# A two-layer diffusion trunk on one core: a second searched order of the same instructions on the five engine queues

## The chip, the cores and the metric

The kernel runs on one core of one Trainium2 chip. The metric is the device time of one execution, in microseconds (us); the median of several runs counts. The names of the engines in this text are those of the profile: PE (TensorE's matmuls; PEld its weight loads), DVE (VectorE), ACT (ScalarE), POOL (GpSimd) and SP (SyncE, which here only issues DMA transfers).

## The reference, cut to what matters

512 latent tokens and 256 context tokens of width 1024 go through two layers. Each layer has a mixer and a gated feed-forward part with a three-tap convolution along the tokens (ConvFFN, width 2816). The mixer of layer 0 is neighbourhood attention on a 64-wide grid for half of the width and spatial gating for the other half; that of layer 1 is retention in both directions. Every part is normed before and after, and shift, scale and gate come from the conditioning vectors (adaLN). Only the latent tokens leave the last layer.

```python
for i in range(DEPTH):
    ctx_out = i < DEPTH - 1
    mod_lat = (silu_c @ ada_w[i] + ada_b[i])[:, None, :]
    mod_ctx = (silu_cc @ ada_w[i] + ada_b[i])[None, None, :]
    sh1, sc1, g1, sh2, sc2, g2 = jnp.split(mod_lat, 6, axis=-1)
    ...
    h_lat = modulate(rmsnorm(x, norm_g[i, 0]), sh1, sc1)
    h_ctx = modulate(rmsnorm(xc, norm_g[i, 0]), csh1, csc1)
    y_ctx, y_lat = hybrid_na_sgu(...)  or  retention_mixer(...)
    x = x + g1 * rmsnorm(y_lat, norm_g[i, 1])
    h = modulate(rmsnorm(x, norm_g[i, 2]), sh2, sc2)
    x = x + g2 * rmsnorm(conv_ffn(h, ...), norm_g[i, 3])
    # the same for xc while ctx_out
```

All inputs and the output are float32.

## The kernel before, in words

**Precision.** Every large product is made of three passes on TensorE: each operand is split into a high and a low part, and high·high, high·low and low·high are added in PSUM (`mm3`, lines 277 to 280). `split` (lines 233 and 234) makes the parts: ACT copies the rounded high part (L233), DVE subtracts it from the source for the low part (L234). So each weight block of 128x1024 that comes by DMA costs ACT about 1.05 us and DVE about 1.22 us before its matmuls can run. The feed-forward and retention projections use block products of a Strassen kind (tiles px, py, pz, xv, yv, zv), whose sums are made on DVE.

**Stages.** The tokens are six tiles of 128 rows: 4 and 5 are context, 0 to 3 latent. From the start: first norms and the modulation vectors (`ad`, L328, native float32 matmuls on blocks `ar` of the modulation weights; transposes of the normed tiles `ht`, L2136), spatial gating and attention of layer 0 (to about 345 us), its output projection and the norms behind it (to 430), the feed-forward part of layer 0 (to 875), the norms between the layers (875 to 945; tiles with the letter c), retention (to 1400), the norms behind it (1400 to 1430; letter d), the feed-forward part of layer 1 (to 1757) and the last norms.

**Norms.** `ssq` (L493) squares half a row tile on ACT and sums it. `rms` (L498) adds the two sums in a 128x1 operation on GpSimd, and `rsq` (L479) raises the result to −1/2, also 128x1 on GpSimd. DVE and ACT then scale the tile (L515 at the start, L531, L543 and L544 later). Each norm is thus a chain ACT, GpSimd, GpSimd, DVE or ACT, and behind it PE transposes the result (`ht` L642 and L2136, `htc` L577) and `split` makes `hb` or `h0c`/`h1c`.

**Background work.** The remaining modulation vectors are made on DVE in small steps (`ada_half`): GpSimd clears an accumulator `acc` (L407), a row of the bias comes by DMA (L408), and DVE adds scaled weight rows to it (L416, 256 operations of 754 ns). Sums of retention weights for the block products are made by DMA alone: copies within DRAM and adding DMAs (`weight_sums`, L380; tiles tv and tq, 512 or 256 KB each), issued by SP and GpSimd and used only in the second layer.

**The order of the work.** `queue()` (lines 2152 to 2174) sets it. The program is built in some order; then the string ORDER (lines 51 to 185) is unpacked. It holds, for each of the five queues, one permutation of that queue's instructions, as the distance of each instruction from the one before it. Each instruction is tied to its predecessor in the permutation, so that the program is emitted in that order:

```python
at += 1 + (z // 2 if z % 2 == 0 else -(z + 1) // 2)
if last is not None:
    self.tc.add_manual_dep(lane[at], last.name, sync, reason="queue")
last = lane[at]
```

The dependency is one of order only; it adds no semaphore. The waits between engines follow from what the instructions read and write. An instruction at the head of a queue that waits holds up everything behind it in that queue, and DMA issues stand in the queues of SP, GpSimd and ACT like any other instruction. The permutations were made by a search program outside the kernel, with a model of the engines; the kernel holds only its result.

**Lines that the steps below touch.** First loads `first_load` (called on line 2208, tiles xn04, xn05) and `first_x` (L515); `ada_first` (L328); `ada_half` (L407, L408, L416); `rms` and `rsq` (L498, L479); `split` (L233, L234); `weight_sums` (L380).

Of the kernel before, what the change touches and what calls it, by code (L numbers as in the profile page):

```python
# [18 lines left out]
P = 128  # L19
D = 1024  # L20
KD = 8
NT = 4
NC = 2
TL = 512
TC = 256
FF = 2816
# [25 lines left out]
c-oD82e>3xb>_LZLRY8i?&_TTb-$c*&N<JE6W+XelXKRLq#0?XQ2?QcB!r|<0wj`z1j3jo8zF&=iN@I8{V+Dci@{)w*WNYjyx#v*zmW!P?{1G?b$4~$Tl  # L52
b#upZ}bDOGJ3-4&6a2`2+auBJw4Y2})BU$iI=Hlaui0C-U+ox{i}xkNq3PV?-w2`D<0J6>$~9?E`O~sNY$ir_wHJr;{hBulMcZZQ|`>YprL?JPp*<?lkW
bbdQ+t<O{mCzb>kifu{v|w$<GsioJ6u4fQyjyF+-tDIOB7R63IEbVdGFd`G-PJk6KYTzn2~=;DQz(@|Pl?u>0bD>ep)2C3`h2gC=(v8nFe-G|82-9z*_@
mWEoo)+pEe?+`X96m(Ul<g#o78jz~zB9Diow$)G(OvGPfn49d+eP~<Ii}{x=}D*3eG587WF#RK)gr?gWvM|PF><>@ZdYYh<w&e@WVnW?oT{jNXy43qS?O
FdQCc=RMY)nuswkf#N>Mh$GpiWP^;PVnf&PkkEPh~)rir#>`sfHG(}F8X&d_p64qeTiDWffCh_0vUnKNe-wdH3MD^-<5v5D~;*AmHwhV>XFcVD<zJxe#!
g~h51h5T}T{+3ItR9jj`yQ*t0(Q17IEkLhrt!?FabCW7D0I5j4IrPdZTBoksRl?<af?MbzagN7VN?Z8M>>OpX5Q(jg^0`u~pwg99Oe4K{uDX6Fjw{z^@>
IXNLbM}~xoxEuYNQFvzM^d%(tw)p7WattQ)4wf^xNV^QA#~~_U_qB8#UE69qrA>H*8H$PucgW=!deLrD15MN^hko1t=eeN%{jdE=s|=2Kw!><5~+gI^|v
QussI+9&gZcx!HnkJHBeyY)C#6y_i1JXB!pmJytZ~5Px|@oX0T|Eq;S!iq>b4+wOvB|0(_+4q-$$-*oeV(9O4r`nlPrMrvv1f7`6#kzpbXnp&r<R@(eX9
YoE9V{04E)i?AUA!_M4(bCgRY|{`d#7K0x7uGtogo%uejx8(>duVxhga(I-gW%teR8{_n$MgxwiovU{mK`sdXrt-&I|YU@Ni(-@p+Y`1gFAJZzHyqGY^K  # L60
Y%ULKFmHa2xtWBzq<qWK=`tgNc7D_4&nsOqEcjkcO<bawK@$=<cP+B$0ai1@iU(?Z+le=g`0v`8aAfe$?<j#C5QxAPt1Ct~?g9R33SLlrkH_7A{D>imHl
=5p0@v&U1jw@@vW9Q&W*zY1!Zrn%H&^P#5%-IO|N>0cEui9^|2o)oj65q?tR;}f3{xb=zm3eq5_EuRv16ea(F{DgQz93(n;fG1qBeFx<WbnXqYOtzljP;
8krIb{@uWKwNrj;b@%M4pilu_DL$JbMaW%h38fwc4NGF6a*Nh*%ipFXyha&piknxfg%$74H#@QMBjp#rhS9;x7gLLgc?9{#C5M2Zw(VbF*`^J8*bT{H`G
1ABeZhw@Ln^ZFD1jMXbW`j?>jwCquy{+E!ILdG2Ac?|Jcn{EnEJZloO*(>HHklY^6u=e7|=Z@3Y1dZ(=J^Isg^*gZC?!c0Q9%ZFq&W<6hb5vE{~V{x#Nu
0LNi0ipwt(G5fwsdr?9cJ;z95-g&9`{~-(!XggSGi1DZ#sDNxs+vl?wIyWZ(KbFiPJ=~vAbO`bOn`Ps@d0tan1f1ZrtcJYh|{N7K#vQ5;N9X;F-Qw=?%K
MdoOiz}=<h}AYl8k&?7JfV8EAdx<oWT>qdRxkCxpA#T6|G_MCjx6d2x-9O79Td^D30~b@4U8&-21NF>VWJ`0VCYnKK66a_N>!0|Wg79}x6mL5B{rgLeiw
A`Q@)vu8Tk<L7!`5+4-<{o4U6bi-4^q35`H6MY=_IB}A0y$qr4S7a}Ia)_?Gs;lw}qK(}|YdhZ((XV_;xfm|k2O1eq+U(P@c+MHm!9Yjg=Pe<2<`|$mN7
<4$8#AInjy2UlQL6or_?Z|S`WNwI!Qh%t;@qbN)XqP~9)nnu9~YP#ZpCh1;3oKMxn?K~ydE!YU><bg?3o>eI86pCd?VSnc~yPGTe^pT(x@A#-DiV3#c^N
2Dw#!GEP|fJ(xUPxAdXG4WU>lCSKdP_t7dtMwr!=E@(PFu&8rv>Rc|%GTBYV>BH7x;5C<b_u`-@Ic3-EFvoW?JM5)Vr;<5cF%9?$r-zQp{ZLz5d57qcdH
>u7RkK0>XX8$Y3MW7-FocS&DGd6g8fOB3?qa9EHwc!wER}Xy_Up?ytF&6SHsm3tHcv5K&v862!!IPni92H&?4ZH3Y_X*k#!R#WkImk9ljyl>q+WkCfIEU  # L70
GJkLc%dx3&eXt;a1~K`a&E%+Y&A!M<H=e0*Yx?iUjiM30M)izMReGQ2MIBSBvi)crkCcSZL6K-?v(4h`HRD?ced1qktdPtbP-4E-qgv8S(>I(`Nsf)MZv
ynPN=)I)vszYtH#-Obgzn>pa{-PZ@2Fu3hIw)?J#y(j6|an`Gc`$Tj@5dD-`+C#4k(myReBZ$w>5-sMscjd_KayM61B$CE+;{9T9&J{tF2kg;~I#tV+NI
+_PdSkUBkr*E7qRC(wyda9`#$KH4?t#6sMFKCkt<kPTlHMo3D#(56AbBEXv;jwLYb`6Kq!*(jT1_aE`{4@|86AIzxJx`JQXT8NCf5L}@x<NYTzL?Y1!kO
vu(z=6A<^5!TwA3J@~;74f;DVLUN-ecXtNO>HoAjG{RrtZt&)1Wd&bGvGl^(S3p<&M#sY=>^Y9#CeW0A;?b&A9OXFSd2C`3YncvIC+McA2$c3F9k=Eghs
-|k^9}zGH0NZIyBbqB=OM|&M3VD@SJg}pRa$Cz&giu&*dj`D4U>_mN0z{Y<5w?&3ZNCv7Kx@%4$)Uc}tnM+<p-q<?;VI>mPPV60brflwa`nbBtMLi&qQ>
Q=x{BTqc+R%1Nva%a1azgT(xQP_ym!~=SSuxa3teEt{S=Zk*1u!0$iv~pk;W#53t+^9q7bV<I4^CU`H1)}L0b{;)pSa|OPq~Ha=Uxu<xP#|ZZ_NYV{aEu
BNDw$(8(w>H?WFaNsiqknUFU52zi{<g|gCIohw)3#n5fG-P9PGp!x(Gzz7*kv|1a$oNWE5%*!0W-PII34UL~%S|*Gbv6w31TcP0{gJ>0V;!@3DwNw*=Vj
HLyxY`}8q9x8Ml6AG9B0z?CY?0=ZhoM#&Y>1)9EUeHNs9S4En3}Vs1)1PkxR6{J8@(d-PA~~8Z5$h=p-}jW*f|BQKZH~u{3H$_dA`AxW?!3$Io|Y?cv3t
pEJ`Io=<<b7IOh-e%(765r%}5tr#qTyF3+>7sb*@}NY0sB2q3q(uvkl>{<hX37<thyPwhq5V36TbkW8Du9~xq8O>d`xbZdP2C^a|N6evQYprexq+vC~s3
1(s&yNA75nCI|ZV32Jr+uC+%fc;A?TWW~(!8Rh%2)x>xu34%=ph%XwDP6j)k&^LP_v&k6gZ7>-jv)UY@g)I9`kL53&`(`JY`DP&?XUy<gxmGB*s=X_5hl  # L80
ZQ=z+<hcfk`>s?P>m%Tjt-(1I7Af`CTH8W%X&G7ahv(ozH9GYY(k=P`_m@|VO{h2c*c@k+=9hC(TJ*se~AxLMtz`zbOH6pL2t=_p;e2vhMRlvKft%|voz
_r`=&V$Cfbbf|>^1OYV`UyDXy7PP)=-MLx|$%Vop@Xs<%Eocj}5~{qNxxj**h4wUuo3k7wW~oH7okpT|B(0Ce$&OllCpJXGd{XS~2~3CfnpeaN0(=mp;B
hgz=tmkh<wrIdGzLB15kH4gIHxb><{01Kqg7iJc4r1oojyfpDL*}91t+I6xTugv?i=;A7xEMNd?C=BpBUc(^rb{8=C!-Td6&5CEaxx{ND6^ybokj|5fR-
u5r8XM{au~rlof0*%eqEs+2s!aHU@`k>*goMgAIerMr)YTj=Z0O*?uY@x8bPXpKD9_%t+KrxsJ&i#u@TcMXQgZ`Ho5tB6Tm-c{1c5qFRnXDbts=gOW{I&
~CVHc;|2h^S;#(f?fCSr^Nsb1jviP%)p^q!DIJ`kY3w%W+z-AeC+r!Hkf#GJB~c>DDG_qnIok;yVOu>qLR%q!qL`nW+=`PIvS~f&|x4*9c_0wFyl1f-d;
aBJkv--wryRc?1{c~H$}7f1<6er`5KeG1m~Oxj#@kFlfyfhk@-ig)IRE~I`DSZ`K{TwGnuEdtu*AavYBv2xi?u3{nk{2;JBE@3`di|J=hEYIy>6{bMyeU
QVodrFs0`Z(<|G|w~3jV<}n(s=njYasAROPv&QEGn}0ym7hniX-2C}A-|$E(;I~>bwA7~8uC8?G_55FWdL{<=r@5RH{ySS!L<30ZlVWd)e&KeJp=52FZr
# [2265 lines left out]
```

## Time and profile before

| | |
|---|---|
| median of 3 runs | 1772.27 us |
| lowest and highest | 1771.36 and 1775.65 us |
| the profiled execution | 1771.19 us, its span 1769.4 us |
| granted TensorE clock, mean over the span | 0.996 |
| busy: PE, PEld, DVE, ACT, POOL | 1731.5, 1563.9, 1434.4, 1122.4, 448.2 us |
| moved by DMA | 330.6 MB, mean 187 GB/s |
| instructions in the trace | 29634 |

The span runs from the first to the last record of the profiled execution; its own time is 1.8 us longer. Busy times add up instructions of one engine, overlapping ones once. An instruction's row gives its start, its length, engine, line, operation, output and inputs, and in brackets the idle time of its engine before it and what ended that. Rows of waits give, for an engine and line, for which producer it waited, the sum, the count and the longest. A window's row gives its length and each engine's busy time within it.

### The profile page before, as it was taken

What the parts mean: (1) busy time and instruction counts of PE and PEld (TensorE: products, weight loads), DVE (VectorE), ACT (ScalarE), POOL (GpSimd) and SP (SyncE); (2) the same over time, 40 slices, a digit from 0 to 9 for tenths busy, and PEclk for the clock granted to TensorE, in tenths of its full rate; (3) what the DMA queues carried; (4) which work ended last, traced back from release to release, by engine and by line L of the source; (5) the groups of instructions that cost most, each with busy time, mean ns of one, the idle gap of its engine ahead of it and who ended that gap; (6) DMA issues with size and microseconds to landing.
All of it is one profiled execution on the core that took longest, in us unless ns stands there. A gap on an engine that the chain in (4) does not pass through costs nothing.

```text
span 1769.4 us, 29634 instructions
## 1 busy us (share of the span) xinstructions
PE 1731.5 (98%) x11108; PEld 1563.9 (88%) x11108; DVE 1434.4 (81%) x2408; ACT 1122.4 (63%) x2046; POOL 448.2 (25%) x570
## 2 busy tenths in 40 slices
PE   7999999999999999999999999999999999999998
PEld 3798888789999899999889999999999889999997
DVE  3887787899888899878998677567657899998887
ACT  6633567786655565665675566566666677767774
POOL 1111344232143333232231131222121110222222
PEclk9999999999999999999999999999999999999999
DMA  8555584679799999999972465656564425787773
GB/s 299 153 163 177 162 200 107 192 217 240 223 205 231 222 246 229 270 230 250 316 206 71 175 172 155 148 133 163 120 151 144 174 103 169 194 219 186 177 159 125
DMA packets 121292, 330.59 MB, mean 187 GB/s; under 512 B 14222, under 2 KB 36238, under 8 KB 120476
## 3 DMA queue, kind: packets, MB, share of 16 engines
q1 hardware_dynamic: 63004, 233.73, 39.5%
q0 software_dynamic: 55840, 86.57, 29.7%
q10 hardware_dynamic: 2304, 8.39, 1.2%
q8 instruction: 87, 1.43, 0.3%
q14 instruction: 57, 0.47, 0.1%
HBM read 256.29 MB, written 98.30 MB: 200 GB/s over the span
## 4 chain that ended last, share of the span: by engine, by line
PE 81%; DVE 7%; ACT 4%; DMA 3%; POOL 3%; issue 2%; DVEq 0%; ACTq 0%; SPq 0%; POOLq 0%
PE px L277 10%; PE wf L278 4%; PE wf L279 4%; PE wf L280 4%; PE xv L277 4%; PE py L277 4%; PE px L280 1%; PE px L278 1%; PE px L279 1%; PE yv L277 1%; PE py L278 1%; PE py L280 1%; PE py L279 1%; PE ug L278 1%; PE wr L278 1%
## 5 line engine op out<-in xcount | busy, mean ns | idle before, releaser
L416 DVE SCALAR_TENSOR_TENSOR acc<-ar,cs,acc 128x512 f32<-128x512 f32 x256 | 188.0, 754 | 9.8 <-DMA acc<-in_adab_row 7.4
L2039 POOL DMA_DIRECT2D yf<-yp x64 | 55.7, 940 | 258.4 <-ACT yp L2035 226.6
L2035 ACT COPY yp<-wf 128x512 f32<-128x512 f32 x118 | 68.6, 584 | 70.5 <-PE wf L280 68.6
L277 PE MATMUL px<-hs,wc 128*128 128x384 f32 (+1 forms) x480 | 112.0, 309 | 0.8 <-ACT pre L1879 0.8
L277 PE MATMUL px<-blk,wb 128*128 128x384 f32 (+1 forms) x480 | 109.0, 308 | 0.0
L1892 DVE SCALAR_TENSOR_TENSOR cv<-pre,cw,cv 128x769 f32<-128x769 f32 (+1 forms) x88 | 77.6, 884 | 27.8 <-ACT cv L1891 27.5
L1891 ACT ACTIVATE cv<-pre,cw 128x770 f32<-128x770 f32 (+1 forms) x88 | 81.3, 926 | 19.3 <-DVE pre L1884 14.0
L277 PEld LDWEIGHTS px<-hs,wc 128*128 128x128 f32 x480 | 82.5, 188 | 6.7 <-ACT pre L1879 1.9
L277 PEld LDWEIGHTS px<-blk,wb 128*128 128x128 f32 x480 | 81.8, 188 | 4.7 <-ACT pre L1879 0.4
L1879 ACT ACTIVATE pre<-px 128x256 f32<-128x256 f32 (+2 forms) x160 | 54.3, 368 | 43.7 <-PE px L277 30.5
L2039 POOL DMA_DIRECT2D yd<-yp x48 | 47.4, 1020 | 124.7 <-ACT yp L2035 122.1
L1895 DVE SCALAR_TENSOR_TENSOR cv<-pre,cw,cv 128x769 f32<-128x769 f32 (+1 forms) x88 | 77.4, 884 | 1.3
L277 PE MATMUL px<-hs,wd 128*128 128x384 f32 x240 | 72.0, 338 | 0.0
L277 PE MATMUL py<-blk,wc 128*128 128x384 f32 x240 | 69.6, 337 | 0.0
L2039 POOL DMA_DIRECT2D yd<-ypg x48 | 45.7, 1006 | 86.5 <-ACT ypg L2035 73.4
L233 ACT ACTIVATE wb<-s 128x512 fp32r<-128x512 f32 x80 | 48.6, 627 | 22.1 <-PE px L277 19.1
L233 ACT ACTIVATE wc<-q 128x512 fp32r<-128x512 f32 x80 | 49.0, 629 | 17.6 <-PE px L277 6.9
L234 DVE TENSOR_TENSOR wb<-s,wb 128x512 fp32r<-128x512 f32 x80 | 54.6, 688 | 4.7 <-ACT wb L233 4.3
L234 DVE TENSOR_TENSOR wc<-q,wc 128x512 fp32r<-128x512 f32 x80 | 54.6, 688 | 4.3 <-ACT wc L233 4.0
L278 PE MATMUL wf<-fo,g 128*128 128x512 f32 x144 | 54.6, 397 | 1.2 <-ACT g L233 1.2
L280 PE MATMUL wf<-fo,g 128*128 128x512 f32 x144 | 55.5, 395 | 0.0
L279 PE MATMUL wf<-fo,g 128*128 128x512 f32 x144 | 55.2, 395 | 0.0
(1735 smaller groups left out, 6895.0 us busy)
## 6 DMA issues: line engine op xcount, KB each, us to landing
ar<-in_adaw SPq DMA_DIRECT2D x96, 512.0 KB, 4.9
yf<-yp POOLq DMA_DIRECT2D x64, 256.0 KB, 4.8
tv<-in_ret_vg SPq DMA_DIRECT2D x28, 512.0 KB, 6.1
yd<-yp POOLq DMA_DIRECT2D x54, 256.0 KB, 6.3
yd<-ypg POOLq DMA_DIRECT2D x54, 256.0 KB, 7.0
tv<-in_ret_vg POOLq DMA_DIRECT2D x14, 512.0 KB, 10.0
tq<-in_ret_qk SPq DMA_DIRECT2D x14, 512.0 KB, 6.2
tv<-tv POOLq DMA_DIRECT2D x14, 512.0 KB, 8.1
```

Of the source, the lines that this page charges most:

```text
L233: self.S.activation(hi, src, AF.Copy)
L234: self.V.tensor_tensor(out=lo, in0=src, in1=hi.bitcast(F32), op=ALU.subtract)
L277: mm = lambda *p, **k: self.T.matmul(*p, skip_group_check=True, **k)
L278: mm(out, lhs[0], rhs[0], start=first, stop=False)
L279: mm(out, lhs[0], rhs[1], start=False, stop=False)
L280: mm(out, lhs[1], rhs[0], start=False, stop=last)
L416: V.scalar_tensor_tensor(out=acc[s], in0=raw[:, kk * 512 : kk * 512 + 512], scalar=self.cs[:, 8 * s + k : 8 * s + k + 1], in1=acc[s], op0= ...
L1891: S.activation(d, s, AF.Identity, scale=w1, bias=b)
L1892: V.scalar_tensor_tensor(out=d[:, 1:W], in0=s[:, 0 : W - 1], scalar=w0, in1=d[:, 1:W], op0=ALU.mult, op1=ALU.add)
L1895: V.scalar_tensor_tensor(out=d[:, 0 : W - 1], in0=s[:, 1:W], scalar=w2, in1=d[:, 0 : W - 1], op0=ALU.mult, op1=ALU.add)
L2035: S.copy(v, ps)
L2039: G.dma_start((yd[t] if first else y[t])[:, o], v, accum_op=ALU.add)
```

## The change

Only the string ORDER differs: 134 lines become 137. Built, the kernel has the same instructions, the same tiles and the same dependencies between engines; the five permutations are others. The author's words for it: the orders were searched anew with a model in which short GpSimd operations wait for VectorE's work on SBUF, and the first loads and norms were reordered.

```diff
 LANES = ("PE", "DVE", "Activation", "Pool", "SP")
 ORDER = """
-c-oD82e>3xb>_LZLRY8i?&_TTb-$c*&N<JE6W+XelXKRLq#0?XQ2?QcB!r|<0wj`z1j3jo8zF&=iN@I8{V+Dci@{)w*WNYjyx#v*zmW!P?{1G?b$4~$Tl
...
 """
```

Unpacked, the two strings compare like this:

| queue | instructions | at another place | furthest forward | furthest back |
|---|---|---|---|---|
| PE | 10964 | 8661 | 80 places | 72 places |
| DVE | 2344 | 1542 | 26 | 24 |
| ACT | 1910 | 1116 | 18 | 18 |
| POOL | 566 | 329 | 19 | 46 |
| SP | 484 | 282 | 35 | 20 |

Nearly all queues are unchanged in what ran from 680 to 770 us and mostly so from 1575 to 1650; from 1727 us on (for SP from 1679, for POOL from 1697) both orders are the same. The places that matter below, old order against new:

```
start, SP     old: ar000 cc xn04 xn05 acc041 xn00 ng ident xn01 adab ar001 ar100 xn02 xn03
              new: xn04 cc xn05 ident ar000 xn00 xn01 adab acc041 ng ar001 xn02 ar100 xn03
start, PE     old: ad(ar000) x4, ht of xn04 x2, ht of xn05 and xn04 x6, ad(ar001), ht x4, ad(ar001) x3, ht x8
              new: ht of xn04, ad(ar000) x2, ht x5, ad(ar000), ht x5, ad(ar000), ad(ar001) x4, ht x6
start, POOL   old: ... rms, rsq of xn04; rms, rsq of xn05; memset acc040; rms, rsq of xn00
              new: ... rms, rsq of xn04; rms, rsq of xn05; rms, rsq of xn00; ...; memset acc040

583-602, POOL old: memset acc110, row acc110, tv24, yd1, memset acc111, row acc111, yd2, yd3 x2, yd2
              new: memset acc110, memset acc111, row acc110, row acc111, yd2, yd1, tq34, yd3 x2, yd2

891-904, POOL old: yc1r, memset acc140, tv47, wxc1, xc1r, wyc2, yc2r, wxc2, wyc3, xc2r, yc3r
              new: yc1r, wxc1, xc1r, wyc2, yc2r, wxc2, xc2r, wyc3, yc3r, wxc3, xc3r
893-904, DVE  new: h1c(hc20) 3 places earlier, h1c(hc21) 2 earlier, scale of xtv 4 later, the rest within 2

1403-1419, DVE  old: yr22, yr11, xd1 x2, sa, yr22, sa x2, yr22, xd1r-scale, yr22, sa, yr33 x2, wp101 low,
                     sa x2, xd2, hb1 low, xd2, yr33, wp011 low, hb1 low, sa, yr33, sa, hb1 low, xd3 x2
                new: yr11, xd1 x2, yr22, sa x4, yr22, xd1r-scale, yr22, wp101 low, yr33, yr22, hb1 low,
                     yr33, xd2 x2, wp011 low, yr33, sa, hb1 low, sa x2, yr33, xd3 x2, xd2r-scale, hb1 low
```

Issues of the background copies move most. On SP, for instance, tv31 goes from 165.8 us (its time in the profile before) to behind what was issued at 78.2, tv11 from 165.2 to 98.2, tq11 from 189 to 135.8, tq34 from 428 to 344.3, tv13, tv23 and tv43 to behind what was issued at 266.5; on POOL two adding DMAs, tv46 and tv47, go from 880.9 and 892.4 to behind work of 1034 and 981.

271 lines of the change are left out of this document (137 added, 134 removed).

## The prediction

> **What bounds the kernel now.** I read the page first (busy shares), then the windows by stage (where the bound stops being full), the chain of waits of PE, and last the timelines around its longest waits.
>
> ```profile
> PE   1731.5 (98%) x11108; PEld 1563.9 (88%) x11108; DVE 1434.4 (81%) x2408; ACT 1122.4 (63%) x2046; POOL 448.2 (25%) x570
> ```
>
> TensorE's matmuls fill 98% of the span, so they are the bound, and an order can't shorten them. What it can win is PE's idle time, and the windows say where that is (columns: window, its length, then busy time of PE, PEld, DVE, ACT, POOL, the granted clock, DMA share, GB/s).
>
> ```profile
> 4.90:19.77 14.87, 10.63 (x36) 4.47 (x36) 3.33 (x5) 7.80 (x23) 5.18 (x9) 0.77 1.00 382
> 25.00:430.00 405.00, 401.75 (x2469) 339.07 (x2468) 331.88 (x692) 255.75 (x539) 107.59 (x147) 1.00 0.66 181
> 430.00:590.00 160.00, 160.00 (x831) 147.15 (x831) 140.16 (x201) 93.44 (x161) 52.53 (x70) 1.00 0.93 221
> 590.00:605.00 15.00, 12.92 (x70) 11.78 (x69) 11.32 (x18) 8.04 (x15) 3.40 (x4) 1.00 0.85 236
> 605.00:875.00 270.00, 270.00 (x1409) 245.75 (x1408) 236.00 (x339) 160.71 (x275) 83.88 (x96) 1.00 1.02 251
> 875.00:945.00 70.00, 64.58 (x456) 58.78 (x455) 63.14 (x102) 49.28 (x100) 25.85 (x33) 1.00 0.64 189
> 945.00:1400.00 455.00, 450.60 (x3345) 426.05 (x3345) 314.66 (x529) 286.87 (x451) 92.97 (x113) 1.00 0.55 148
> 1400.00:1430.00 30.00, 25.51 (x163) 22.31 (x162) 28.24 (x53) 24.66 (x57) 9.74 (x14) 0.94 0.52 179
> 1430.00:1455.00 25.00, 24.38 (x201) 23.77 (x200) 25.00 (x39) 19.25 (x37) 0.00 (x0) 1.00 0.20 65
> 1455.00:1757.00 302.00, 301.45 (x2093) 278.82 (x2094) 270.80 (x424) 208.84 (x375) 61.45 (x72) 1.00 0.69 175
> ```
>
> PE's idle time (length less PE busy): 4.2 us in the start, 3.3 in 25 to 430, 2.1 in 590 to 605, 5.4 in 875 to 945, 4.4 in 945 to 1400, 4.5 in 1400 to 1430, 0.6 and 0.6 after that: 25 us of 1771, the ceiling of any reordering. In 430 to 590 and 605 to 875 there is none; there an order can only lose. The waits name the causes:
>
> ```profile
> PE pz L280 <- DVE wa L234: 2.1, 1, 2.1
> PE rkc L280 <- DVE rwk L234: 2.0, 1, 2.0
> PE pf L278 <- ACT hb L233: 1.7, 1, 1.7
> ...
> PE pf L279 <- DVE hb L234: 1.2, 2, 1.0
> ...
> PE rn L280 <- DVE h1c L234: 1.1, 1, 1.1
> ...
> PE ht L642 <- ACT yr L544: 0.9, 1, 0.9
> PE htc L577 <- DVE hc L588: 0.8, 1, 0.8
> ...
> PE wf0C L278 <- DVE fin L768: 0.4, 1, 0.4
> ```
>
> **The change part by part.** The five orders are permutations of the old ones: no instruction, dependency or wait comes or goes, so PE's 1731.5 us stay, and each cost is a wait that shrinks, grows or moves. Where I say that a waiting matmul has more PE work ahead, I counted the matmuls queued before it in both orders at their durations in the trace: more work ahead covers the wait, less lengthens it.
>
> *Start.*
>
> ```profile
> 4.95 3.42 PE L328 MATMUL ad<-ar,cs 128*2 128x256 f32 x8 [4.95 <-ACT cs L285]
> 11.16 0.44 PE L2136 MATMUL ht<-ident,xn 128*128 128x128 f32 x2 [2.79 <-DVE xn L515]
> 13.00 1.54 PE L2136 MATMUL ht<-ident,xn 128*128 128x128 f32 x6 [1.40 <-DVE xn L515]
> ...
> 18.75 1.09 PE L2136 MATMUL ht<-ident,xn 128*128 128x128 f32 x8
> ```
> ```profile
> 7.83 0.63 ACT L493 ACTIVATE jx<-xn 128x512 bf16<-128x512 f32 x1 [2.94 <-DMA xn<-in_x]
> ```
> ```profile
> 10.35 0.75 DVE L515 TENSOR_SCALAR xn<-xn,x04r 128x1024 f32<-128x1024 f32 x1 [10.35 <-POOL x04r L479]
> ```
> ```profile
> ident<-in_ident SPq DMA_DIRECT2D x1, 64.0 KB, 6.7
> ```
>
> SP used to issue the modulation block ar000 first and token tile xn04 third; now xn04 is first, xn05 third, then ident, then ar000. The first 512 KB issued were in by 4.95 (the matmuls that read ar000 start), the next by 7.83, and further ones follow at 512 KB/382 GB/s = 1.4 us. So xn04 gains 2.9 us: squared, through GpSimd and normed it takes 3.3 us (7.83 to 10.35 + 0.75), ready at about 8.2 instead of 11.1. ident (6.7 us from an issue near 2.3) lands at about 9. xn05 arrives at 7.8 and is normed by about 11.3. ar000 is now the third large load: 9.3 to 10.9, the later end if ident's issue holds the queue. PE thus loses the ad passes that ran from 4.95 in dead time, and gains the waits of 2.79 and 1.40. Its 10.63 us of work up to 19.77 run unbroken from about 9.7. At cold durations that would end at 19.9, no gain. But the transposes took 0.26 us each at 13.00 and 0.14 at 18.75: the clock rose within 5.75 us of the start of the unbroken stretch. Counted so from 9.7 it rises at 15.45, with 10.63 − 0.44 − 5.75 = 4.4 us left that take 2.2: the stretch ends at 17.7, a gain of 2.1. If the clock rises at 18.75 as before, the gain is 0.4; if ar000 lands at 10.9 as well, a loss of 0.2. I take −1.5, range −2.5 to +0.2; from 25 us on PE has 99% busy, so it is kept.
>
> ```profile
> 33.56 3.62 PE L328 MATMUL ad<-ar,cs 128*2 128x256 f32 x16
> ```
>
> The ad passes show the two rates: 3.42/8 = 0.43 us at 4.95, 3.62/16 = 0.23 here. The Trainium skill (TensorE: Matmul & The Clock Gate, Part 1: The HAM clock gate) has the clock released after about 3.4 us of sustained matmuls. Counted from 9.7 that would be 13.1, and the start would gain about 3.2 instead of 1.5; the trace here needed 5.75, so I stay with the trace.
>
> *25 to 430.* Of the eleven longest waits five have more PE work ahead (up to 4.5 us), five less (up to 1.8), one the same. Waits that lengthen do so only if their producer isn't moved up too, which it mostly is. I take −1.0 of the 3.3, range −2.5 to +1.5.
>
> *590 to 605.*
>
> ```profile
> 583.92 0.54 POOL L408 DMA_DIRECT2D acc<-in_adab_row  x1 [0.30 <-POOL acc L407]
> ...
> 588.18 0.53 POOL L408 DMA_DIRECT2D acc<-in_adab_row  x1 [0.30 <-POOL acc L407]
> ```
> ```profile
> 595.38 1.54 DVE L416 SCALAR_TENSOR_TENSOR acc<-ar,cs,acc 128x512 f32<-128x512 f32 x2 [3.57 <-DMA acc<-in_adab_row]
> ...
> 601.55 1.22 DVE L234 TENSOR_TENSOR wa<-f0011r,wa 128x1024 fp32r<-128x1024 f32 x1
> ```
>
> DVE waited 3.57 us for the second of two bias rows, and the low half of wa behind it made PE wait 2.1 us. The new GpSimd order does both memsets before both row issues. The second memset waits for a split on DVE, so the first row too is issued at about 588 instead of 584 and lands near 595. DVE waits for the first row then, about as long, with the rest of the queue behind it; pz has 1.2 us more PE work ahead, but wa's low half stands later. I take 0, range −2.1 (the wait gone) to +1.0.
>
> *875 to 945.*
>
> ```profile
> 900.21 0.30 POOL L498 TENSOR_SCALAR wxc<-ssxc 128x1 f32<-128x1 f32 x1 [2.96 <-ACT jxc L493]
> 900.82 2.54 POOL L498 TENSOR_SCALAR wyc<-ssyc 128x1 f32<-128x1 f32 x1 [0.31 <-DVE hc L588]
> 903.45 0.56 POOL L479 TENSOR_TENSOR xc2r<-wxc,mhalf 128x1 f32<-128x1 f32 x1
> ```
> ```profile
> 904.55 1.41 DVE L531 SCALAR_TENSOR_TENSOR fin<-yf,yc3r,fin 128x512 f32<-128x512 f32 x2 [1.35 <-POOL yc3r L479]
> ```
>
> The same one-column operation takes 0.30 us on a free GpSimd and 2.54 while DVE runs splits and additions back to back. The new order puts xc2r straight behind the short wxc, so it no longer waits out the 2.54: about 901.2 instead of 904.0. The matmul rn that waited 1.1 has 1.05 us more work ahead and its h1c comes three places earlier: gone. wf0C (0.4) has 0.8 more: gone. htc (0.8) has 0.25 more. Together −1.75, less 0.35 for two later waits with that much less ahead: −1.4. The long wait, rkc 2.0, stays: wyc's slow operation now begins after xc2r, yc3r comes at about 901.2 + 2.54 + 0.56 = 904.3, and DVE waits for it as before. Range −3.4 (rkc gone too) to +0.7 (twice the 0.35).
>
> The Trainium skill (SBUF — State Buffer, section SBUF: two separate sides) has VectorE operations with two SBUF inputs and GpSimd exclude each other for whole instructions, whichever comes first. By that a short operation waits for at most one VectorE instruction; wyc's 2.54 us covers about four. By the rule yc3r would be out before DVE gets there, DVE's 1.35 and most of rkc's wait would go, and the sum would be 1.3 lower.
>
> *945 to 1400.* Four waits have 0.5 to 1.7 us more ahead, four shorter ones 0.2 to 0.8 less, the rest about the same. I take a quarter of the 4.4: −1.1, range −2.5 to +1.0.
>
> *1400 to 1455.*
>
> ```profile
> 1415.05 1.65 POOL L498 TENSOR_SCALAR wxd<-ssxd 128x1 f32<-128x1 f32 x1 [5.34 <-ACT jxd L493]
> ```
> ```profile
> 1412.84 0.69 DVE L234 TENSOR_TENSOR hb<-sa,hb 128x512 fp32r<-128x512 f32 x1
> ```
> ```profile
> 1417.91 0.72 ACT L544 ACTIVATE yr<-xd,xd2r 128x512 f32<-128x512 f32 x1 [1.30 <-POOL xd2r L479]
> ```
>
> DVE's copies out of PSUM and hb's low half go up four places, ahead of two additions, so hb comes about 1.5 us earlier (PE waited 1.7 and 1.0 for its halves); the scale of xd comes two places earlier, so xd2r and yr follow (0.9). But DVE is busy 28.24 of 30 us here and 25.00 of the next 25: what is moved up pushes something else down, and the stage can win only what DVE itself idles. I take that, 30 − 28.24 = 1.8: −1.8, range −4.0 to 0.
>
> *Stretches without idle.* Background copies (512 KB, DRAM to DRAM) move by up to 140 us, several in front of weight or modulation loads in SP's FIFO. SP waits for nothing there but a full queue; behind a copy stand the loads, and behind these ACT's and DVE's splits.
>
> ```profile
> tv<-in_ret_vg SPq DMA_DIRECT2D x28, 512.0 KB, 6.1
> ```
>
> At the 251 GB/s of 605 to 875, where the DMA engines are full, a copy ahead of a load costs it 512 KB/251 = 2.1 us; most loads are issued far enough ahead. I take +1.0 for half of one, range 0 to +4.2 (two in full).
>
> Sum: −1.5 − 1.0 + 0 − 1.4 − 1.1 − 1.8 + 1.0 = −5.8 us. The profiled execution took 1771.19 us (span 1769.4), 1.1 below the median 1772.27 of the runs and 0.2 below the lowest. 1771.19 − 5.8 = 1765.4.
>
> **The rivals.** *The waits move, none goes.* For it: DVE is full at 1430 to 1455 and has 63.14 of 70 at 875 to 945, and rkc and pz wait on chains that the order leaves whole. Against: most waits at 875 to 945 and in 1410 to 1419 have their producer moved up by places that I could count. It gives the start at 0.4, 875 to 945 and 1400 to 1455 at half (−0.7, −0.9), the rest 0 and the +1.0: −1.0, 1770.2. *Loads late behind copies, slower.* The mechanism of the last term, where PE has no idle time to hide it: each load that comes late in full costs 2.1 us. From the third such load (6.3) the gains are gone; slower by over 0.3% takes more than 5.3 + 5.8 = 11.1 us, the sixth. With seven, 1765.4 + 14.7 = 1780. For it: the DMA share of 1.02 in 605 to 875. Against: the trace before has copies in the same queue in that stretch, and PE idles nowhere in it. *The edit doesn't do what it says.* No wait on DVE is added; GpSimd still runs when its inputs are in, so 2.54 us operations can recur at other places. If they hit a row like yc3r's twice more (2.2 each over 0.30), the sum is −1.4: 1769.8, a case of no change. *More is won:* rkc and pz go too: −5.8 − 2.0 − 2.1 = −9.9, 1761.3.
>
> **How the numbers follow.** A measurement here tells about 0.3% (5.3 us) from no change, so faster is below 1767.0. My forecast (sum between −9 and −4) has 0.45, more won 0.14, waits moved 0.20, GpSimd's slow operations again 0.11, loads late 0.10, of which 0.07 beyond 0.3%. Faster: 0.14 and nine tenths of 0.45, as the sum's edge is only 1.6 from the bound: 0.54; slower 0.07; the same 0.39. All best ends together would give 1754, all worst ones about 1780; they won't fall together. The range, 1757.5 to 1773, leaves out about one in ten on each side.
>
> **What would show it.** In the changed profile: first transposes of xn04 at about 9 and no idle over 1 us on PE from 11 to 20; rkc's wait still there, rn's gone; a wait of DVE for a bias row near 590; hb's waits shorter by 1 us each and DVE still full to 1455; PE busy 1731 in all; no idle in 430 to 590 and 605 to 875. The forecast is wrong if PE idles there, or if the idle of 875 to 1455 comes out as large as before.

## The result and the profile after

The changed kernel is faster: 1760.45 us in the median of four runs (1758.47 to 1761.47) against 1772.86 us before (1771.36 to 1775.65), a ratio of 0.9927 with a 95% interval of 0.9910 to 0.9944. That is 12.4 us. The forecast was 1765.4 with a range of 1757.5 to 1773.0. The profiled execution took 1759.8 us, with a span of 1758.0. Two of the eleven runs of one kernel below (the start and the copies), at 2838.72 and 4372.51 us, are slow ones and count in no ratio.

The windows of the changed kernel by stage (columns as before; the clock stands third from the right). Stages now start some microseconds earlier, so the same clock times hold slightly later work.

```profile
590.00:605.00 15.00, 15.00 (x81) 13.92 (x80) 14.45 (x22) 8.19 (x12) 4.76 (x5) 1.00 0.97 254
605.00:875.00 270.00, 268.32 (x1390) 242.36 (x1389) 232.46 (x334) 161.00 (x281) 83.31 (x99) 1.00 1.00 250
875.00:945.00 70.00, 67.31 (x485) 62.52 (x484) 64.09 (x104) 50.73 (x100) 18.71 (x26) 0.98 0.49 153
945.00:1400.00 455.00, 451.14 (x3345) 427.46 (x3344) 322.00 (x538) 291.03 (x466) 96.82 (x123) 1.00 0.56 153
1400.00:1430.00 30.00, 28.31 (x222) 27.25 (x221) 29.52 (x53) 23.75 (x50) 3.23 (x6) 0.94 0.35 125
1430.00:1455.00 25.00, 23.36 (x168) 21.55 (x167) 25.00 (x39) 20.54 (x39) 0.00 (x0) 1.00 0.43 126
```

The chain of waits of PE in the changed kernel:

```profile
PE ht L2139 <- DVE xn L518: 7.6, 1, 7.6
PE px L280 <- ACT pre L1882: 2.6, 2, 1.6
PE pf L281 <- ACT hb L236: 1.4, 1, 1.4
PE ag L440 <- ACT ah L236: 1.3, 1, 1.3
PE htc L580 <- ACT fin L547: 1.1, 1, 1.1
PE htc L580 <- DVE fin L546: 1.1, 1, 1.1
```

The waits of pz (2.1), rkc (2.0) and wf (1.2) are gone, and rn's (1.1) is down to 0.2. In their place stand px (2.6), ag (1.3) and two of htc (2.2), which the profile before did not have in that size. These rows give back about as much as they take, and the idle time in the windows of 945 to 1400 fell by only 0.5 us. They don't explain 12 us.

What does is a measure that I did not use in the prediction. For each matmul record, take the time from its start to the next record's start, and take off the median of that time for its shape. The sum of the medians is the same for both kernels, so the two can be compared where equally much matmul work has been done. The lead of a kernel over the one before, in microseconds, at the places named by the times of the kernel before:

| at (us) | 25 | 430 | 590 | 605 | 650 | 875 | 945 | 1400 | 1455 | end |
|---|---|---|---|---|---|---|---|---|---|---|
| changed kernel | 3.0 | 5.2 | 5.4 | 7.7 | 5.2 | 4.8 | 6.4 | 11.9 | 11.8 | 11.6 |
| start alone (below) | 3.0 | 3.9 | 1.0 | 2.4 | 1.9 | 1.8 | 0.5 | 0.4 | −0.6 | −0.4 |
| retention alone (below) | 0.4 | 0.3 | −0.3 | 1.6 | 1.6 | 1.6 | 0.2 | 5.1 | 4.2 | 4.2 |

Each row is one execution. A lead is read as its change over a stage: the changed kernel gained 3.0 in the start, 2.2 to 430, 2.3 at 600 and lost 2.5 of it by 650, gained 1.6 in the norms between the layers and 5.5 in retention, and nothing behind it. The forecast was 1.5 for the start, 1.0 to 430, 0 at 600, a loss of 1.0 in the stretches without idle time, 1.4 for the norms, 1.1 for retention and 1.8 behind it. One term, retention, makes most of the difference.

Executions of the same order differ, too. Each kernel below, the port kernel apart, has the old or the new order in each stage, so the change of the lead over a stage can be set side by side for the two orders (us; least, median, most; the number of executions in brackets; kernels that alter the stage in yet another way are left out):

| stage | old order | new order |
|---|---|---|
| up to 25 | −0.3, 0.2, 1.9 (5) | 1.7, 2.8, 3.0 (6) |
| 590 to 605 | −2.3, 1.2, 1.9 (6) | 2.2, 2.3, 2.3 (6) |
| 875 to 945 | −1.4, −1.4, 0.0 (7) | 1.1, 1.5, 2.5 (6) |
| 945 to 1400 | −0.1, 0.0, 0.4 (4) | 4.9, 5.2, 5.5 (4) |
| 1400 to 1460 | −1.0, −0.8, 0.0 (8) | −1.0, −0.6, 0.2 (5) |

Against the usual execution of the old order, then, the gain is near 2.6 in the start, 1.1 at 600, 2.9 in the norms, 5.2 in retention and none that can be told behind it. The trace of before was an unlucky execution at 600 and a lucky one in the norms. Only retention has a spread that is small beside its gain.

### The profile page after: what moved, and what is told of

Its sections match the earlier page's. It is cut to its first block, busy times and chain, and to the rows that moved or that the text cites. A ratio compares the mean times of both kernels' runs of the same rounds, so it can differ in the third digit from the quotient of the medians.

```text
span 1758.0 us, 29651 instructions
## 1 busy us (share of the span) xinstructions
PE 1727.7 (98%) x11108; PEld 1565.2 (89%) x11108; DVE 1438.6 (82%) x2408; ACT 1122.7 (64%) x2047; POOL 440.4 (25%) x570
## 4 chain that ended last, share of the span: by engine, by line
PE 89%; DVE 5%; ACT 2%; issue 1%; DMA 1%; POOL 1%; DVEq 0%; POOLq 0%; ACTq 0%
PE px L280 12%; PE wf L282 5%; PE wf L281 5%; PE wf L283 5%; PE xv L280 4%; PE py L280 4%; PE px L282 2%; PE px L281 2%; PE px L283 2%; PE yv L280 2%; PE py L283 1%; PE xk L280 1%; PE py L281 1%; PE py L282 1%; PE ug L283 1%; PE pz L281 1%
```

## The experiments

My theory was that the gains are local: each comes from the order within its stage, and they add up. The rival was that they come from what a stage takes over, above all from where the background copies are issued. Within the stages, the question was which of the changed orders does it, and whether GpSimd's collisions with VectorE have a part in it. Times are device times against runs of the kernel before made beside them; single runs are read by their profile alone.

**The start alone.** All five queues in the new order up to about 28 us, the old order behind it.

```diff
-PE[0:70] DVE[0:12] ACT[0:28] POOL[0:14] SP[0:14] in the old order
+PE[0:70] DVE[0:12] ACT[0:28] POOL[0:14] SP[0:14] in the new order
```

> The new order for the start alone (all five queues up to about 28 us), the old order behind it. Measured at equal matmul work, the changed kernel stood 3.0 us ahead at 25 us. If the gains are local to the stages (my theory), this kernel keeps that lead to the end: about 3.0 us faster than the kernel before, the other stages as before, rkc's wait of 2.0 and the pz wait of 2.1 still there. Rival: an earlier start only meets later waits on loads and norms that come no earlier; then the lead shrinks to under 1.5 us by 200 us and the total is within 1 us of before.

The lead of 3.0 us at 25 us came again and held until 430. The ratio is 0.9985 (0.9971 to 0.9998; medians 1769.42 and 1773.26). The profiled execution, at 1771.77 one of the slower of the twelve, lost 2.8 us at 434 and more later; the median of the timed runs kept it. By the timed runs the gain of the start stands by itself, though the interval ends just short of no change; the profiled execution lost it at a wait behind a transfer at 434, which the experiment on the copies below takes up.

**Retention alone.** The new order between 945 and 1386 us, the old one around it.

```diff
-PE[5158:8430] DVE[1290:1797] ACT[1026:1444] POOL[363:474] SP[290:389] in the old order
+PE[5158:8430] DVE[1290:1797] ACT[1026:1444] POOL[363:474] SP[290:389] in the new order
```

> The old order up to 945 us and from 1386 us, the new one between (retention alone). At equal matmul work the changed kernel gained 5.5 us there, where I had forecast 1.1. If that gain comes from the order within the stage, this kernel gains 5 to 6 us there and is about 5.5 us faster than before. Rival: it comes from what is carried in (background copies that were issued elsewhere, queues further ahead after 875 to 945); then at most 2 us of it shows here.

The ratio is 0.9973 (0.9961 to 0.9985; medians 1767.72 and 1773.26), and the lead went from 0.2 to 5.1 us within the stage. By groups of matmuls, the time above the medians fell for ro from 3.4 to 0.9 us, for xv from 2.7 to 0.0 and for rt from 2.6 to 1.3; in the changed kernel these are 0.8, −0.1 and 1.3. A new wait of ag takes 1.4 back in both. So the gain of retention comes from the order within it, and not from what is carried in.

**One copy behind the bias rows.** The old order with one transfer of GpSimd's queue moved.

```diff
 POOL: memset acc110, row acc110,
-tv24 (copy), yd1, memset acc111, row acc111,
+yd1, memset acc111, row acc111, tv24 (copy),
 yd2
```

> The old order with one transfer moved: the background copy tv24, which GpSimd issued between the two bias rows at 584.7 us, stands behind the second row. My prediction said that the wait at 590 comes from the second memset, which waits for a split on DVE; then the row's wait of 3.57 us on DVE and pz's 2.1 us on PE stay. The rival reads the changed trace otherwise: the row landed 7.2 us after its issue before and 3 us after it in the changed kernel, where no copy stands ahead of it. By that the DVE wait falls to under 1.5 us and pz's wait to under 0.5 us, a gain of about 2 us at 605 us.

GpSimd's rows and VectorE's, in this kernel:

```profile
588.00 0.54 POOL L404 DMA_DIRECT2D acc<-in_adab_row  x1 [0.30 <-POOL acc L403]
588.65 1.03 POOL L376 DMA_DIRECT2D tv<-tv  x1
```
```profile
590.27 2.99 DVE L412 SCALAR_TENSOR_TENSOR acc<-ar,cs,acc 128x512 f32<-128x512 f32 x4
```

The row is issued at 588.00, as late as before (588.18), and yet DVE's four steps run from 590.27 without a break: the wait of 3.57 us is gone, and with it the wait of pz (the lead rose by 2.3 us from 590 to 605). Before, the median time from issue to landing of the two rows was 6.6 us in that stretch, here 5.0. The second memset still waits for DVE here (1.98 us). So it isn't what made the row late, though my prediction had it so, but the copy between the rows. In all six executions with the copy between them DVE waited 1.7 to 3.8 us for the second row, and in this one not at all. The size is another matter: pz waited 2.1 us in the trace of before, but 0.2 to 2.8 in the five others (median 0.9). The retention kernel, with the same order here, shows one of the short waits:

```profile
593.83 1.54 DVE L414 SCALAR_TENSOR_TENSOR acc<-ar,cs,acc 128x512 f32<-128x512 f32 x2 [1.69 <-DMA acc<-in_adab_row]
```

So some 1.1 of the 2.3 us belong to the order.

**GpSimd's product behind another.** The new order with one pair of GpSimd's queue exchanged.

```diff
 POOL: swk3, yd0r, yd0r,
-e03, e03 (diagonal), swq3
+swq3, e03, e03 (diagonal)
```

> The new order with one pair swapped on GpSimd near 1097 us: the product with sin for q (swq3) ahead of the two products that make e03. In the changed kernel the addition ks on DVE took 2.68 us there instead of 0.69, and PE waited 1.5 us for ag behind it. If GpSimd's product of two SBUF tiles holds DVE's operation with two SBUF inputs, the addition falls to 0.7 to 1.4 us and the wait of ag falls under 0.5 us, a gain of about 1 us at 1110 us, with the collision moved to the q products. Rival: the addition waits for something else (its inputs from ACT or GpSimd come late); then it stays at over 2 us.

The addition in question in the changed kernel, GpSimd's queue beside it, and the same addition in this kernel:

```profile
1096.38 2.68 DVE L1522 TENSOR_TENSOR ks<-ks,swk 128x512 f32<-128x512 f32 x1
```
```profile
1096.86 1.65 POOL L1509 TENSOR_TENSOR e<-e,e 128x384 f32<-128x384 f32 x1
1098.59 0.79 POOL L1510 TENSOR_TENSOR e<-e,ident 128x128 f32<-128x128 f32 x1
```
```profile
1096.71 0.69 DVE L1518 TENSOR_TENSOR ks<-ks,swk 128x512 f32<-128x512 f32 x1
```

With GpSimd's two products elsewhere the addition takes 0.69 us (0.69 as well in the two kernels below that share the exchange, 2.67 to 2.68 in all four profiled ones that have the new order here without it), the wait of ag is gone, and the lead over the changed kernel at 1150 us is 1.6 us larger against 1100. The run took 1759.95 us; 0.9 us of the gain was lost again at 1400 to 1455. So VectorE can be held by GpSimd, and the new order has places where it is.

**Two repairs of the new order.** The exchange above, and the copy tv44 moved from in front of two transfers out of the buffer yp to a gap 8 us earlier.

```diff
 POOL: yd4,
+tv44 (copy),
 yd5, yd5,
-tv44 (copy),
 yd0, yd0
```

> The new order with two changes on GpSimd's queue: swq3 ahead of e03 near 1097 us as before, and the adding copy tv44, which stood at 615.8 us just ahead of two transfers yd out of the buffer yp, moved five places earlier, behind yd4 at 607.6. In the changed kernel ACT waited 3.1 us for yp at 631 and PE 2.0 us behind that. If the copy ahead of yd delays the release of yp, these 2.0 us of PE go, and the total is 3 us below the changed kernel (with the 1.5 of ag), near 1757. Rival: the transfers are limited by the DMA engines in that stretch (share 1.00), so that the wait only moves to another buffer; then the stretch 605 to 650 stays 2 us slower than 590 to 605 left it, and the total is within 1.5 us of the changed kernel.

ScalarE's copy into yp in the changed kernel, and here:

```profile
631.14 0.58 ACT L2038 COPY yp<-wf 128x512 f32<-128x512 f32 x1 [3.08 <-DMA yd<-yp]
```
```profile
628.66 0.59 ACT L2034 COPY yp<-wf 128x512 f32<-128x512 f32 x1 [0.26 <-PE wf L279]
```

The wait for the transfer is gone, and the lead at 650 us is 7.1 instead of 5.2. The ratio is 0.9915 (0.9900 to 0.9931; median 1758.83), against 0.9927 for the changed kernel: its interval overlaps, and 1.5 us of the 1.9 came back as a wait of px at 790. The warm kernel below has the old place of the copy and waited only 1.21 us for yp there, two other kernels with the old place 2.62 and 2.79, so part of this wait belongs to the execution.

**A warm clock at the start.** The new order with nine matmuls of a zeroed tile in front (PE's result is overwritten).

```diff
+for _ in range(9):
+    T.matmul(ps[:, :256], self.wm[:, :P], self.wm, start=True, stop=True)
 for kp in range(2):
```

> The new order with nine matmuls of a zeroed tile put ahead of all other PE work (result overwritten, nothing else changed), so that PE is busy from about 1 us on instead of from 7.6. If the start is set by the TensorE clock, which came up 4.5 us after PE's work began in the changed kernel (10.4 at half rate to 13.2 at full), the first transposes and modulation matmuls run at full rate, and PE is 1 to 2 us earlier at 25 us. Rival: the start is set by the arrival of xn04, xn05 and ar000; then PE waits for xn05 instead and less than 0.5 us is gained.

PE's first rows in this kernel:

```profile
1.18 6.84 PE L319 MATMUL ad<-wm 128*128 128x256 f32 x18 [1.18 <-DVE wm L284]
7.85 0.27 PE L2140 MATMUL ht<-ident,xn 128*128 128x128 f32 x1
8.44 1.02 PE L332 MATMUL ad<-ar,cs 128*2 128x256 f32 x4 [0.32 <-DMA ar<-in_adaw]
...
10.44 0.77 PE L2140 MATMUL ht<-ident,xn 128*128 128x128 f32 x5 [0.71 <-DVE xn L519]
```

Four modulation matmuls take 1.02 us instead of 1.86 at half rate, and then PE waits for ar000 and for xn05. From 22 to 35 us the same matmuls start 0.8 us earlier than in the changed kernel, at 43 us 0.15, in part because ug waits 0.3 us at 39 where it did not before. The ratio is 0.9923 (0.9908 to 0.9939): no difference from the changed kernel. So the clock does set a part of the start, and what it gives is all but gone within 20 us.

**The start and the copies.** As the start alone, and SP and GpSimd in the new order up to 463 us.

```diff
-POOL[14:164] SP[14:151] in the old order
+POOL[14:164] SP[14:151] in the new order
```

> The new order for the start on all queues, and for SP and GpSimd up to 463 us (loads and background copies issued in the new places), everything else old. The kernel with the new start alone lost 2.8 of its 3.3 us at 434 us, where ACT waited 4.2 us for a transfer out of yp behind a copy tq. If background copies set that stretch and not the engines' own order, issuing them in the new places keeps the lead: 3 us or more ahead at 480 us. Rival: the loss at 434 belongs to one execution or to the order of DVE and ACT there; then this kernel loses it as well, or the timed median of the start alone was already 3 us below before.

This kernel was 1.7 us ahead at 25 us and 1.0 at 480; it lost 0.3 at 184 and 0.6 at 307, gained 1.7 up to 430 and lost 1.5 at 441. The ratio is 0.9980 (0.9967 to 0.9992), that of the start alone 0.9985. The new places of the copies did not keep the lead by themselves. As the timed medians of both kernels lie 3.6 to 3.8 us below before, the loss at 434 in the start alone is best read as belonging to that execution; no other run was profiled that could show it. What decides it in an execution was not found.

**The order of weight splits in retention.** The old order with rwk behind rwt4 on ACT and DVE, for three heads.

```diff
-ACT, DVE: rwk(h+1), rwt4(h)
+ACT, DVE: rwt4(h), rwk(h+1)
```

> The old order with three pairs swapped on ACT and on DVE, in retention: the split of the next head's rwk behind the split of rwt4, which the next matmuls xv need (before: rwk first, xv waits 0.5 to 0.7 us at 1136, 1198 and 1261). If a part of the 5 us of retention is simply the order of weight splits, the three waits go and the kernel is 1.5 to 2.1 us ahead of before at 1300 us, counted from 1100. Rival: the gain in retention comes from GpSimd's operations meeting less DVE work; then nothing moves, under 0.5 us.

The three waits of xv stood as before, at 0.72, 0.61 and 0.49 us. What they wait for is not the weights, but ACT's copy rg out of the PSUM bank. The run took 1784.71 us: 4.8 us were lost at 375 to 430, 2.3 at 600 and 1.4 in the norms, where its order is that of before, and 4.4 in one place at 1270 that the exchange opened (xv and stl). The theory of the splits falls.

**The shared port.** A kernel for itself that computes nothing of the reference, in the form of the expectation.

```diff
+for k in range(16):
+    op(o[k])                       # VectorE, 128x512
+    if k in (1, 5, 9):
+        short(f"{name}{k}", o[k])  # GpSimd, 128x1
```

> Nothing of the reference is computed (the output is zeros). Alone on the engines: GpSimd's one-column operation of the norms is run four times with DVE idle, then beside 16 DVE operations of 128x512 back to back, first with two SBUF inputs, then with one SBUF input, then with one PSUM and one SBUF input; last, two GpSimd products of two SBUF tiles (128x384) beside DVE additions with two SBUF inputs. If the rule holds that whoever comes first has the shared port for one instruction, the short operation takes 0.30 us alone and beside the last two kinds, and at most about 1.0 us (0.30 and the rest of one 0.69 us addition) beside two SBUF inputs, and one addition is held beside each product (over 1.2 us). My prediction took the other side from the 2.54 us row: a stream of additions keeps the port, and the short operation takes over 1.5 us beside it, up to the end of the stream.

Durations in ns, least/median/most; gal is alone (the longest of the four ran beside the last memset and the first two additions), gss beside additions of two SBUF inputs, gs beside one SBUF input, gsp beside PSUM and SBUF; big are the products:

```profile
L74 POOL TENSOR_SCALAR gal<-a x4: 291/294/2168, 1.5 to 2.6; 128x1 f32<-128x1 f32 x4
L74 POOL TENSOR_SCALAR gss<-o x3: 1114/1184/1185, 4.9 to 9.6; 128x1 f32<-128x1 f32 x3
L74 POOL TENSOR_SCALAR gs<-o x3: 291/292/4757, 13.9 to 19.1; 128x1 f32<-128x1 f32 x3
L74 POOL TENSOR_SCALAR gsp<-o x3: 291/291/292, 19.8 to 24.6; 128x1 f32<-128x1 f32 x3
```
```profile
L95 POOL TENSOR_TENSOR big<-o,b x2: 989/5092/9196, 29.3 to 38.5; 128x384 f32<-128x384 f32 x2
```
```profile
L93 DVE TENSOR_TENSOR o<-a,b 128x512 f32<-128x512 f32 x16 | 9.7, 681 | 0.0
```

The short operation takes 0.29 us alone, 1.1 to 1.2 beside additions of two SBUF inputs, and 4.76 beside multiplications of one SBUF tile: it started at 13.9 and ended at 18.6, as the last of these 16 ended. The product began at 29.3 and ended at 38.5, again only after DVE's stream (its last addition ended at 37.7), while the second, with DVE idle, took 0.99. DVE's additions were never slower (681 ns). The Trainium skill (SBUF — State Buffer, SBUF: two separate sides) has whoever comes first hold the pair for a whole instruction. The short operation beside additions comes near that, 0.2 us above the 1.0 that the expectation worked out. The addition of 2.68 us above fits in kind, though its record begins 0.48 us before that of the product. The other two do not fit: they let more than ten VectorE instructions pass, as if a back-to-back stream kept the port. Why the short operation gets its turn beside additions and the product doesn't, these runs don't show. My prediction's figure of 2.54 us for one beside four additions is not what this kernel shows for that kind of stream (1.2).

**Work between producer and consumer.** The old order, PE's queue alone changed: at three places eight matmuls of other groups moved to just before the waiting xv.

```diff
 PE: ... xv (first half),
+yv, yv, stl, stc, stc, wr x3 (from up to 5 us earlier),
 xv (second half, waits)
```

> The old order with PE's queue alone changed, at three places in retention: eight matmuls of other groups (yv, stc, stl, wr), which stood up to 5 us earlier, moved to between the last xv matmul of one half and the first of the next, which waits until ACT has copied the bank out (0.72, 0.61 and 0.49 us at 1136, 1198 and 1261, each with some 0.1 behind it). If the gain of retention comes from work put between a producer on PE and its consumer on PE, these waits go and the kernel is 1.5 to 2.0 us ahead of before at 1300 us, counted from 1100. Rival: the later yv, stc and wr make ACT and DVE late, and the same time is lost at the next waits; then under 0.7 us is left at 1300.

It went the other way: 7.9 us were lost between 1100 and 1300, at these three places (up to 2.1 us in one piece, from start to start). ACT's queue shows how, and the chain of waits of PE the price:

```profile
1137.05 1.06 ACT L229 ACTIVATE rwt<-rwt43r 128x1024 fp32r<-128x1024 f32 x1 [3.87 <-PE wr L276]
1138.02 0.57 ACT L1462 COPY rg<-xv 128x512 f32<-128x512 f32 x1
```
```profile
PE xv L273 <- ACT rg L1462: 5.1, 3, 1.9
```

ACT waited 3.87 us with the split of the next weights until the moved wr was done, and the copy rg stands behind it in the queue. PE's order can't be changed alone: ACT's queue was laid out for the old one. So the mechanism by which retention gained is argued from the two traces (below), not shown.

**The old order after retention.** The new order with the old one from 1386 to 1458 us (before's times).

```diff
-PE[8430:8864] DVE[1797:1911] ACT[1444:1539] POOL[474:490] SP[389:409] in the new order
+PE[8430:8864] DVE[1797:1911] ACT[1444:1539] POOL[474:490] SP[389:409] in the old order
```

> The new order with the old one from 1386 to 1458 us (before's times). The changed kernel gained nothing there, where I had forecast 1.8. If DVE's work sets that stretch (25.0 of 25 us busy behind it in both kernels), the old order gives the same time: within 0.7 us of the changed kernel between 1386 and 1460. Rival: the new order does win at hb and loses the same at the last px; then the two waits show at their old places, and the stretch differs by over 1 us one way or the other.

PE's waits in this kernel that belong to the stretch:

```profile
PE pf L277 <- ACT hb L232: 2.0, 2, 1.7
PE pf L278 <- DVE hb L233: 1.5, 2, 1.0
PE ht L641 <- ACT yr L543: 1.4, 1, 1.4
...
PE wf L277 <- ACT g L232: 1.2, 1, 1.2
```

They are before's waits, at before's places, where the changed kernel has pf and px. Yet over the stretch the kernel lost 0.8 us against before's trace and the changed kernel 0.1, and 40 us later both are 11.6 us ahead. It took 1759.88 us. These are different waits of nearly the same sum: the difference of 0.7 us lies within what executions of one order differ by here (the table above, −1.0 to 0.2). So the new order wins nothing in this stretch that these runs can tell. That VectorE's work sets it fits with its 25.00 us of 25 in both kernels, but is not shown.

**What helped, together.** The new order with both repairs of GpSimd's queue and eight matmuls of zeros in front.

> The new order with what helped: swq3 ahead of e03, tv44 moved ahead, and eight matmuls of zeros at PE's start. Counted from the runs: 1.5 for ag, 0 to 2 for the wait at 631 (it came in two of three executions of the unchanged place), 0.1 for the start at 50 us. Expected 1.6 to 3 us below the changed kernel, near 1758; with the rival, that DVE-bound stretches behind take the gains back, within 1 us of it.

The median is 1756.01 us (1755.06 to 1757.85, five runs), the ratio 0.9904 (0.9886 to 0.9923): the fastest kernel of this study, and all of its runs lie below every run of the changed kernel. That is 4.4 us below the changed kernel's median, more than expected; the two profiled executions differ by 2.0. The intervals of the two ratios still overlap, as each is measured against its own runs of before.

## Why the prediction came out as it did

The gain came out at twice the sum of 5.8. That the time still lay within the range is in part luck: the start, 590 to 605 and retention gained more than their ranges allowed, and the stretches without idle time and 1400 to 1455 took some of it back. The rival "more is won", given a chance of 0.14, said that rkc's and pz's waits would go too; they did, and its 1761.3 is near the 1760.45 measured. But it left retention at 1.1, so that its number is right by luck as well.

**The ceiling** set the size, and it failed. "25 us of 1771, the ceiling of any reordering" took PE's idle time from the windows; the whole gain stayed under it, but retention's 5.5 exceeds the stage's 4.4. PE busy fell from 1731.5 to 1727.7 us with the same matmuls, where I had said 1731. Busy time covers short waits in two ways: the records overlap (here one lasts 0.28 us, and the next starts 0.12 us after it), and a matmul that waits has a longer record (below, two xv take 0.51 us behind a wait and 0.40 without). From start to start, 945 to 1400 held 13.4 us above the medians, where the window showed 4.4 idle. In the changed kernel it is 7.8.

**945 to 1400** was the mis-sized term, −1.1 against −5.5 measured. The step that failed is the quarter of 4.4, and behind it the counting: I counted PE work ahead of a waiting matmul from the start of the queue. But the chain behind these waits begins on PE itself: xv fills a bank, ACT copies it out, and the next xv needs it. What matters is the work between the two. Before, the trace has one matmul there:

```profile
1135.98 0.28 PE L277 MATMUL xv<-rwt,h1c 128*128 128x256 f32 x1
1136.10 0.28 PE L277 MATMUL yv<-rwt,s1r 128*128 128x256 f32 x1
1136.94 0.51 PE L277 MATMUL xv<-rwt,h0c 128*128 128x256 f32 x2 [0.56 <-ACT rg L1466]
```

The changed kernel has eight (yv, three stc, stl and three more yv), and the second xv follows without a gap:

```profile
1127.35 0.28 PE L280 MATMUL xv<-rwt,h1c 128*128 128x256 f32 x1
1127.47 0.28 PE L280 MATMUL yv<-rwt,s1r 128*128 128x256 f32 x1
...
1127.82 0.28 PE L281 MATMUL stl<-rv,kd 128*128 128x256 f32 x1
1127.94 0.52 PE L280 MATMUL yv<-rwt,s1r 128*128 128x256 f32 x3
1128.30 0.28 PE L281 MATMUL stc<-rv,kd 128*128 128x256 f32 x1
1128.41 0.40 PE L280 MATMUL xv<-rwt,h0c 128*128 128x256 f32 x2
```

My count gave the matmul at 1136 0.2 us less work ahead, and so a longer wait. This is about xv. What shortened the waits of ro (2.6 us) and rt (1.3) was not traced.

**The start** was right in its mechanism and half in its size: −1.5 against −3.0 (against the usual execution of the old order 2.6), where the range ended at −2.5.

```profile
7.64 0.48 PE L2139 MATMUL ht<-ident,xn 128*128 128x128 f32 x1 [7.64 <-DVE xn L518]
8.63 1.86 PE L331 MATMUL ad<-ar,cs 128*2 128x256 f32 x4 [0.51 <-ACT jx L496]
10.42 1.54 PE L2139 MATMUL ht<-ident,xn 128*128 128x128 f32 x6
...
13.17 2.32 PE L331 MATMUL ad<-ar,cs 128*2 128x256 f32 x10
```

ident was there by 7.6 and ar000 by 8.6, earlier than I had put them, and at 13.17 the passes take 0.23 us: the clock was up at most 4.5 us after the unbroken stretch began, where I had taken 5.75. In the warm kernel 13 passes at 0.43 us and five at 0.23 make the 6.84 us of the first row: the clock rose 5.6 us after 1.18. The rule of the Trainium skill (TensorE: Matmul & The Clock Gate, Part 1: The HAM clock gate) that I weighed has 3.4 us of sustained work, which is shorter than either of these. Its 3.2 us for this term was closer than my 1.5.

**590 to 605** was put at 0 and gained 2.3, about half of it because the trace of before waited longer than usual there. The copy between the rows was the cause of the wait (third experiment), and in the new order no copy stands ahead of the rows: issued at 580.3, they let DVE start at 583.65.

```profile
580.30 1.05 POOL L411 DMA_DIRECT2D acc<-in_adab_row  x2
```
```profile
583.65 0.75 DVE L419 SCALAR_TENSOR_TENSOR acc<-ar,cs,acc 128x512 f32<-128x512 f32 x1 [0.47 <-DMA acc<-in_adab_row]
```

Then 2.5 us went behind the wait for yp at 631: the rival of copies ahead of loads, in the stretch that I named, but with one late release of a buffer instead of six late loads. PE idled 1.7 us in 605 to 875, which I had named as a sign that the forecast is wrong. The term also rested on a misreading, "SP waits for nothing there but a full queue". In 605 to 875 SP waited most for buffers that DVE had still to read:

```profile
SPq L219 <- DVE acc L416: 91.5, 23, 11.2
SPq L219 <- DVE wd L234: 64.6, 9, 9.8
```

So a load there can't be issued before DVE frees its buffer, wherever the copies stand.

**875 to 945** came to −1.6 (forecast −1.4), but not as I had it. rn and wf0C went, as said. rkc's wait, which was to stay, went too: wyc took 0.40 us in the place where I had it take 2.54.

```profile
895.00 0.40 POOL L501 TENSOR_SCALAR wyc<-ssyc 128x1 f32<-128x1 f32 x1
```

In exchange htc waits twice for the scaled fin, 2.2 us. Two errors of equal size met, and the agreement is luck in another way, too: five of the seven executions of the old order lost 1.1 to 1.4 us here against the trace of before, in which the clock stayed up (last section). Against these the stage gained about 2.9, twice the forecast.

**1400 to 1455** was put at −1.8 and gave 0. "The stage can win only what DVE itself idles" was right as a bound, and DVE's idle time did go (29.52 of 30 busy). But PE's next wait, px at 1438 (1.6 us), took it: the first rival, in this one stage. **25 to 430** gave −2.2 (forecast −1.0, within its range), and the stretches without idle time lost 0.3 us beside the 2.5 at 631, where I had taken 1.0 in all.

GpSimd's collisions, the point of the search, have a part in it that no run separates: its one-column operations in the norms between the layers take 0.43 us in the median instead of 1.07 (wyc), but retention, where most of GpSimd's instructions stand within three places of the old order, gave the most.

## What to carry to other kernels

Measure what an order can win from start to start of the matmuls, against the median of each shape, and not by idle time: here the first showed three times the second in the stage that mattered. For a wait whose chain begins on the same engine, count the work between producer and consumer, and move all queues of that stage together. Before a stage is credited with a gain, compare several executions of each order there. A background copy in a GpSimd queue belongs behind the small rows and buffer transfers that somebody waits for.

## What the runs showed of the hardware

A wait of PE can cost more than itself. In the windows of 905 to 910 us, the kernel before and the kernel with the start alone have the same order and the same wait of 2.0 us for rkc just ahead:

```profile
905.00:910.00 5.00, 3.00 (x26) 2.84 (x25) 5.00 (x10) 4.61 (x11) 0.95 (x2) 1.00 0.87 302
```
```profile
905.00:910.00 5.00, 4.66 (x27) 4.66 (x27) 4.69 (x10) 4.47 (x9) 0.95 (x2) 0.66 0.77 265
```

In the second the clock fell to 0.66 behind the wait. Of the seven profiled executions with the old order here, all with this wait, five had that, and each lost 1.1 to 1.4 us from 875 to 945 against the trace of before. In the trace of before and the one of the kernel with work between producer and consumer it stayed at 1.00, and they differ by 0.3. The same wait thus cost up to 1.4 us more in some executions. The changed kernel had a fall of its own, behind htc (0.66 from 895 to 900). In the start alone, retention alone and the changed kernel PE was busy for 1.4 of the 3.4 us just ahead of the fall; before has such a stretch too (1.40 us from 904.0 to 907.4), without a fall. The Trainium skill (TensorE: Matmul & The Clock Gate, Part 1: The HAM clock gate) has a free-running window decide. These runs agree in that the same wait does or doesn't bring the clock down.

I had also not expected that a stream of VectorE instructions can keep GpSimd out to its end (4.76 and 9.2 us in the port kernel), nor that one execution in a timed program can lose 4.8 us in a stretch of transfers whose order is the same (375 to 430 us in the kernel with exchanged splits).
